# Up projection of a gated MLP on one Trainium2 core: eight of 22 column pairs made from seven half-size products, with sums on VectorE

## The chip, the cores and the metric

The kernel runs on one core of a Trainium2 chip. Its time is the device time of one execution in microseconds (us). A run is one such time; a kernel's time is the median of its runs. One further execution is taken under the hardware profiler, and every row shown below comes from it. The engines are TensorE (PE, with its weight loads as PEld), VectorE (DVE), ScalarE (ACT), GpSimd (POOL) and SyncE (SP), whose queue issues all the large DMAs of this kernel.

## The reference, cut to what matters

One layer of a trunk with D = 1024, 512 tokens and an inner width of 2816. Token mixing comes first and is not touched. The second half of the layer is:

```python
h = rmsnorm(x) * (1 + scale) + shift          # (512, 1024), adaLN
u = causal_dwconv(h @ w_up)                   # w_up (1024, 5632), width 3 along the tokens
gate, value = split(u, 2)                     # 2816 columns each
x = x + adaLN_gate * ((silu(gate) * value) @ w_down)
```

## The kernel before, in words

Inputs and outputs are float32. The kernel splits each operand of this projection into a high part (a cast to the type that the rows call fp32r) and a low part (the operand less its high part), and a product is made of three matmuls, high by high, low by high and high by low, each with 128 rows of K.

The up projection is the loop over f from 0 to 21 (L1302). Pair f is the gate tile f and the value tile f+22, each 128 columns of `w_up` by 512 tokens. `up` (L1287 to L1293) makes one tile in a PSUM bank: 8 K-tiles by 3 matmuls of 512 tokens, so 48 matmuls a pair. In each of its halves of K the weights come through `load_w`: SP loads 256 KB into `w_st` (three buffers), ACT casts it to `w_hi` (L225), POOL subtracts to get `w_lo` (L227); `w_hi` and `w_lo` have nine slots each, so weights can be ready about two pairs ahead. Pairs 0 and 1 are made in halves of 256 tokens, out of four banks, while the last rows of `h2_hi` and `h2_lo` (the split of h, transposed) come in.

`conv` (L1295 to L1300) follows for each tile: ACT scales it out of PSUM (L1297), DVE adds the two shifted terms (L1298, L1299), each of which reads the bank again. Then ACT takes Silu of the gate (L1325), DVE multiplies (L1326), ACT casts (L1327) and DVE makes the low part (L1328) of the activation, which the down projection reads later. Banks go round a ring of eight (L1282).

At f = 4 and 8 the second adaLN gate is summed on DVE (`gate_steps`, seven L410 rows each), from 256 KB pieces that SP loads between the weights; at f = 6 and 10 it is split, at f = 7 and 11 TensorE sums it over partitions (`gate_end`, L421) and DVE adds it to `g2b` (L423).

The down projection (`down`, L1174 to L1201) loads its weights with `share` 2: every second low part is made on DVE and not on POOL. Each engine takes its instructions in the order in which the program holds them.

Of the kernel before, what the change touches and what calls it, by code (L numbers as in the profile page):

```python
# [27 lines left out]
NF = D_FF // P  # L28
# [108 lines left out]
def hybrid_trunk(ctx, tc, x, vecs, convs, mod_cols, mod_gates, in_first, in_cols, in_fox, in_moba, fox_f_bias, lora,  # L137
                 rwkv_g2, w_out, w_up, w_down, norm_final, out):
    nc = tc.nc
    mm = nc.tensor.matmul  # L140
    V, S, G = nc.vector, nc.scalar, nc.gpsimd
    dma = nc.sync.dma_start
# [76 lines left out]
    def split_w(staged, share=0):  # L219
        st, nkt, n = staged  # L220
        pool, bufs = wpools[0] if len(wpools) == 1 or turn[0] % sum(b for _, b in wpools) < 3 else wpools[1]
        turn[0] += 1
        hi = pool.tile([P, WCOLS], F32R, name="w_hi", bufs=bufs)
        lo = pool.tile([P, WCOLS], F32R, name="w_lo", bufs=bufs)
        (V.tensor_copy if hv[0] else S.copy)(hi[:, :n], st[:, :n])  # L225
        e = V if share and turn[0] % share == 0 else G
        e.tensor_tensor(lo[:, :n], st[:, :n], f32(hi[:, :n]), op=OP.subtract)  # L227
        return [z[:, :n].rearrange("p (k n) -> p k n", k=nkt) for z in (hi, lo)]
# [69 lines left out]
    with tc.manual_schedule(engines=ENGINES):  # L298
# [9 lines left out]
        n = vrows.shape[0]  # L308
# [11 lines left out]
        for k in range(NK):  # L320
            mm(pc[k // 4][:, P * (k % 4):P * (k % 4) + P], cact[:, k:k + 1].to_broadcast([P, P]), ident,
               start=True, stop=True)
# [18 lines left out]
        for k in range(NK):  # L341
# [29 lines left out]
            hi, lo = wk[k]  # L371
            for w, h, last in ((hi, hT_hi, False), (lo, hT_hi, False), (hi, hT_lo, True)):
                for j in range(NFIRST):
                    mm(first[j], w[:, P * j:P * j + P], h[:, k, :], start=k == 0 and w is hi and not last,  # L374
                       stop=k == NK - 1 and last)
# [112 lines left out]
    with mix:  # L488
# [294 lines left out]
        with tc.tile_pool(name="bounce", bufs=1) as bp, tc.tile_pool(name="abp", bufs=1, space=PSUM) as abp, \  # L783
# [10 lines left out]
            for s in range(31):  # L794
                m, w = s + 1, 31 - s
# [285 lines left out]
        for cc in range(NC_):  # L1081
# [19 lines left out]
            pu = bank("ch", [P, 4, 64])  # L1101
# [8 lines left out]
            if cc < NC_ - 1:  # L1110
                pn = bank("ch", [P, 4, 64])
                for j in range(4):
                    for par in range(2):
                        mm(pn[H[par], j, :], BKT[:, j, cc, 64 * par:64 * par + 64], vs[cc][:, par, j, :],
                           start=True, stop=True)
# [37 lines left out]
    late = ctx.enter_context(tc.tile_pool(name="late", bufs=1))  # L1153
    g2b = consts.tile([P, D], F32, name="g2b", tag="cB")
    h2_hi = late.tile([P, NK, T], F32R, name="h2_hi")
    h2_lo = late.tile([P, NK, T], F32R, name="h2_lo")
    def tm(dt=F32):
        return late.tile([P, T], dt, name="tm", bufs=TM)
# [110 lines left out]
    feed.run(UP2)  # L1269


    a_hi = [hbuf.tile([P, NK, T], F32R, name="h_hi"), late.tile([P, NF - NK, T], F32R, name="a_hi")]
    a_lo = [hbuf.tile([P, NK, T], F32R, name="h_lo"), late.tile([P, NF - NK, T], F32R, name="a_lo")]

    def act_tile(arr, f):
        return arr[0][:, f, :] if f < NK else arr[1][:, f - NK, :]

    def cvec(w, f):
        n = 44 * w + f
# [2 lines left out]
    ring = itertools.cycle(("mm", "ch", "at", "mm", "ch", "at", "pv", "ch"))  # L1282

    def up_weights(f):
        return [load_w(w_up[f, q], 4) for q in range(2)]
# [9 lines left out]
    def conv(pu, f):  # L1295
        u = tm()
        S.activation(u, pu, AF.Identity, scale=cvec(2, f), bias=cvec(3, f))  # L1297
        V.scalar_tensor_tensor(u[:, 1:], pu[:, 0:T - 1], cvec(1, f), u[:, 1:], op0=OP.mult, op1=OP.add)  # L1298
        V.scalar_tensor_tensor(u[:, 2:], pu[:, 0:T - 2], cvec(0, f), u[:, 2:], op0=OP.mult, op1=OP.add)  # L1299
        return u  # L1300

    for f in range(NF):  # L1302
        if f == 0:

            pfirst = [bank(t) for t in ("ch", "ch", "at", "at")[:2 * FG]]
            for h in range(2):
                for n, pu in enumerate(pfirst):
                    feed.run(max(0, 6 + 2 * n - len(kept)))
                    up(pu, kept[4 + 2 * n:6 + 2 * n], slice(256 * h, 256 * h + 256))
                    if h == 0 and n < 2:  # L1310
                        norm2_cols(2 + n)
            us = [conv(pu, n // 2 + NF * (n % 2)) for n, pu in enumerate(pfirst[:2])]
        elif f < FG:
            us = [conv(pu, f + NF * n) for n, pu in enumerate(pfirst[2 * f:2 * f + 2])]
        else:
            us = []
            for z in (f, f + NF):
                pu = bank(next(ring))
                up(pu, up_weights(z), slice(0, T))
                us.append(conv(pu, z))  # L1320
        ug, uv = us
        if f == 0:
            LATE.close()
            mixers.close()
        S.activation(ug, ug, AF.Silu)  # L1325
        V.tensor_tensor(uv, ug, uv, op=OP.mult)  # L1326
        S.copy(act_tile(a_hi, f), uv)  # L1327
        V.tensor_tensor(act_tile(a_lo, f), uv, f32(act_tile(a_hi, f)), op=OP.subtract)  # L1328
        if f == 2:
            dma(g2b, gate_bias(40))  # L1330
            nfb = consts.tile([P, D], F32, name="nfb", tag="g1b")
            dma(nfb, norm_final[None, :].to_broadcast([P, D]))
        if f in (4, 8):
            for g in gate_steps(1, f // 8, tm, tm):
                g()
        if f in (6, 10):
            gate_parts(1, f // 10, tm)
        if f in (7, 11):
            gate_end(1, f // 11, bank(next(ring)), g2b)
# [81 lines left out]
```

## Time and profile before

| | |
|---|---|
| time, median of 3 runs | 747.79 us (746.29 to 749.0) |
| the profiled execution's own time | 747.43 us |
| its span, first to last instruction | 745.7 us |
| mean granted TensorE clock | 0.983 |
| pairs 2 to 15, from 396 to 553 us | 157.0 us, PE busy in all of it |

The span is the time between the first and the last instruction; the run is 1.7 us longer. A chain of waits follows the work that ended last back to the start, so its rows are in order of time on one path through the engines. Where a row of instructions says "idle before", it was waiting for what is named behind the arrow.

### The profile page before, as it was taken

What the parts mean: (1) busy time and instruction counts of PE and PEld (TensorE: products, weight loads), DVE (VectorE), ACT (ScalarE), POOL (GpSimd) and SP (SyncE); (2) the same over time, 40 slices, a digit from 0 to 9 for tenths busy, and PEclk for the clock granted to TensorE, in tenths of its full rate; (3) what the DMA queues carried; (4) which work ended last, traced back from release to release, by engine and by line L of the source; (5) the groups of instructions that cost most, each with busy time, mean ns of one, the idle gap of its engine ahead of it and who ended that gap; (6) DMA issues with size and microseconds to landing.
All of it is one profiled execution on the core that took longest, in us unless ns stands there. A gap on an engine that the chain in (4) does not pass through costs nothing.

```text
span 745.7 us, 11381 instructions
## 1 busy us (share of the span) xinstructions
PE 717.4 (96%) x4224; PEld 563.3 (76%) x4224; DVE 422.4 (57%) x761; ACT 350.5 (47%) x671; POOL 300.1 (40%) x262
## 2 busy tenths in 40 slices
PE   6999999999988999999999999999999999999996
PEld 5874767897656766668798888888888888888884
DVE  7957997885997577643645484664344453114114
ACT  8748655454442553535565444354444443223204
POOL 0023744665352312626476544444544522225200
PEclk9999979999997999999999999999999999999998
DMA  8941201337763231214234353633233333232203
GB/s 323 394 165 42 68 19 29 86 100 225 241 193 121 63 123 44 69 46 130 82 100 127 110 178 109 202 102 93 86 102 96 88 107 103 85 99 100 86 13 113
DMA packets 43018, 86.90 MB, mean 117 GB/s; under 512 B 5001, under 2 KB 5203, under 8 KB 42963
## 3 DMA queue, kind: packets, MB, share of 16 engines
q1 hardware_dynamic: 42963, 86.18, 36.4%
q8 instruction: 33, 0.54, 0.3%
q14 instruction: 22, 0.18, 0.1%
HBM read 84.05 MB, written 2.10 MB: 116 GB/s over the span
## 4 chain that ended last, share of the span: by engine, by line
PE 85%; DVE 9%; ACT 2%; issue 1%; DMA 1%; POOL 0%; SPq 0%; DVEq 0%; POOLq 0%; ACTq 0%
PE ch L1290 4%; PE ch L1293 4%; PE ch L1291 4%; PE mm L455 3%; PE at L1290 3%; PE at L1293 3%; PE mm L1290 3%; PE mm L1293 3%; PE at L1291 3%; PE mm L1291 3%; PE mm L456 2%; PE mm L457 2%; PE ch L374 2%; PE ch L1185 2%; PE ch L1184 2%; PE ch L1183 2%
## 5 line engine op out<-in xcount | busy, mean ns | idle before, releaser
L227 POOL TENSOR_TENSOR w_lo<-w_st,w_hi 128x512 fp32r<-128x512 f32 (+1 forms) x164 | 220.1, 1346 | 340.1 <-ACT w_hi L225 318.6
L225 ACT CAST w_hi<-w_st 128x512 fp32r<-128x512 f32 (+1 forms) x184 | 112.9, 617 | 167.9 <-PE at L1185 44.7
L227 DVE TENSOR_TENSOR w_lo<-w_st,w_hi 128x512 fp32r<-128x512 f32 x22 | 16.1, 734 | 83.8 <-ACT w_hi L225 83.8
L1290 PE MATMUL ch<-h_hi,w_hi 128*128 128x512 f32 (+1 forms) x152 | 55.2, 372 | 1.3 <-ACT h_hi L1234 1.3
L1291 PE MATMUL ch<-h_hi,w_lo 128*128 128x512 f32 (+1 forms) x152 | 54.9, 369 | 0.0
L455 PE MATMUL mm<-h_hi,w_hi 128*128 128x512 f32 x104 | 48.8, 469 | 1.8 <-ACT ptr L1017 1.8
L456 PE MATMUL mm<-h_lo,w_hi 128*128 128x512 f32 x104 | 42.2, 406 | 0.0
L457 PE MATMUL mm<-h_hi,w_lo 128*128 128x512 f32 x104 | 42.2, 405 | 0.0
L1290 PE MATMUL at<-h_hi,w_hi 128*128 128x512 f32 (+1 forms) x104 | 36.2, 360 | 0.0
L1291 PE MATMUL at<-h_hi,w_lo 128*128 128x512 f32 (+1 forms) x104 | 36.1, 359 | 0.0
L1293 PE MATMUL ch<-h_lo,w_hi 128*128 128x512 f32 (+1 forms) x152 | 35.0, 371 | 0.0
L1290 PE MATMUL mm<-h_hi,w_hi 128*128 128x512 f32 x88 | 34.7, 394 | 0.0
L1291 PE MATMUL mm<-h_hi,w_lo 128*128 128x512 f32 x88 | 34.6, 393 | 0.0
L1290 PEld LDWEIGHTS ch<-h_hi,w_hi 128*128 128x128 f32 x152 | 28.6, 188 | 7.1 <-ACT h_hi L1234 1.8
L1298 DVE SCALAR_TENSOR_TENSOR tm<-ch,vec,tm 128x511 f32<-128x511 f32 x17 | 12.7, 749 | 36.7 <-ACT tm L1297 36.7
L1291 PEld LDWEIGHTS ch<-h_hi,w_lo 128*128 128x128 f32 x152 | 28.6, 188 | 5.2
L430 DVE SCALAR_TENSOR_TENSOR w_m<-w_m,cB 128x512 f32<-128x512 f32 x32 | 25.8, 831 | 9.7 <-DMA w_m<-in_mod_cols_dram 9.6
L1293 PEld LDWEIGHTS ch<-h_lo,w_hi 128*128 128x128 f32 x152 | 26.7, 188 | 5.5 <-POOL h_lo L1235 0.2
L455 PEld LDWEIGHTS mm<-h_hi,w_hi 128*128 128x128 f32 x104 | 20.3, 195 | 9.0 <-issue 3.1
L1006 ACT ACTIVATE pr<-at,mx 128x128 f32<-128x128 f32 (+3 forms) x32 | 16.9, 527 | 21.6 <-DVE mx L1004 21.1
L1325 ACT ACTIVATE tm<-tm 128x512 f32<-128x512 f32 x22 | 13.9, 633 | 25.6 <-DVE tm L1299 25.6
L1004 DVE TENSOR_REDUCE mx<-at 128x1 f32<-128x128 f32 (+3 forms) x32 | 15.6, 488 | 17.3 <-PE at L1001 17.1
(472 smaller groups left out, 1850.3 us busy)
## 6 DMA issues: line engine op xcount, KB each, us to landing
w_st<-in_w_up_dram SPq DMA_DIRECT2D x88, 256.0 KB, 2.7
w_st<-in_w_down_dram SPq DMA_DIRECT2D x44, 256.0 KB, 2.6
wm<-in_mod_cols_dram SPq DMA_DIRECT2D x16, 512.0 KB, 10.0
w_m<-in_mod_cols_dram SPq DMA_DIRECT2D x32, 256.0 KB, 3.7
w_st<-in_in_cols_dram SPq DMA_DIRECT2D x30, 256.0 KB, 2.7
w_m<-in_mod_gates_dram SPq DMA_DIRECT2D x16, 256.0 KB, 3.0
w_st<-in_w_out_dram SPq DMA_DIRECT2D x16, 256.0 KB, 2.6
tm<-in_mod_gates_dram SPq DMA_DIRECT2D x16, 256.0 KB, 4.7
```

Source lines behind the costliest of these rows:

```text
L225: (V.tensor_copy if hv[0] else S.copy)(hi[:, :n], st[:, :n])
L227: e.tensor_tensor(lo[:, :n], st[:, :n], f32(hi[:, :n]), op=OP.subtract)
L374: mm(first[j], w[:, P * j:P * j + P], h[:, k, :], start=k == 0 and w is hi and not last, stop=k == NK - 1 and last)
L430: V.scalar_tensor_tensor(wm, wm, 1.0, cB[:, cols], op0=OP.mult, op1=OP.mult, accum_out=acc2[:, z, k, half:half + 1])
L455: mm(out[0], hi[:, z, :], hT_hi[:, k, :], start=k == 0, stop=False)
L456: mm(out[0], hi[:, z, :], hT_lo[:, k, :], start=False, stop=False)
L457: mm(out[0], lo[:, z, :], hT_hi[:, k, :], start=False, stop=k == NK - 1)
L1004: V.reduce_max(mx[:, 0:1], s_ps[:, :n], axis=AX.X, negate=True)
L1006: S.activation(pr[:, :n], s_ps[:, :n], AF.Exp, bias=mx[:, 0:1], accum_out=mx[:, 1:2])
L1290: mm(pu[:, tok], hi[:, k % 4, :], h2_hi[:, k, tok], start=k == 0, stop=False)
L1291: mm(pu[:, tok], lo[:, k % 4, :], h2_hi[:, k, tok], start=False, stop=False)
L1293: mm(pu[:, tok], w[k // 4][0][:, k % 4, :], h2_lo[:, k, tok], start=False, stop=k == NK - 1)
```

## The change

Pairs 5, 6, 8, 9, 11, 12, 14 and 15 are made by `up_seven`. It sees a pair as a two by two block product: the two halves of K, the two halves of the tokens, and the gate and value columns. Four half-size blocks of the weights (`a11`, `a12`, `a21`, `a22`) and of h make the result in seven products in place of eight. Each product has 4 K-tiles by 3 matmuls of 256 tokens; so 84 matmuls of 256 replace 48 of 512. The blocks of h are summed and differenced once, by `half_sums` at f = 2 and 3 (tiles `s`, `a0`, `a1`, `a2`, high and low). The weights of such a pair are combined on DVE in place in their staging tiles `w_st4`, which have four buffers, just the four tiles of one pair; seven split weights come of them, with `share` 2. Three partial results are copied out of PSUM by ACT (`snap`, `snap5`) and two adds on DVE put them together in PSUM. The arrays that hold the activations from pair 16 on are allocated later.

```diff
+SEVEN = (5, 6, 8, 9, 11, 12, 14, 15)
+NA = 16
...
+    sums = [[late.tile([P, 4, 256], F32R, name=n + p) for p in ("hi", "lo")] for n in ("s", "a0", "a1", "a2")]
...
+    def half_sums(c):
+        x = {}
+        for q in range(2):
+            for h in range(2):
+                x[q, h] = tm().rearrange("p (k t) -> p k t", k=2)
+                part = (slice(0, P), slice(4 * q + 2 * c, 4 * q + 2 * c + 2), slice(256 * h, 256 * h + 256))
+                (V if h else G).tensor_tensor(x[q, h], f32(h2_hi[part]), f32(h2_lo[part]), op=OP.add)
+        t1, t3, t2, t4 = x[0, 0], x[0, 1], x[1, 1], x[1, 0]
+        V.tensor_tensor(t1, x[0, 1], x[0, 0], op=OP.subtract)
+        V.tensor_tensor(t3, x[1, 1], x[0, 1], op=OP.subtract)
+        V.tensor_tensor(t2, x[1, 1], t1, op=OP.subtract)
+        V.tensor_tensor(t4, x[1, 0], t2, op=OP.subtract)
+        for z, t in zip(sums, (t1, t2, t3, t4)):
+            S.copy(z[0][:, 2 * c:2 * c + 2, :], t)
+            G.tensor_tensor(z[1][:, 2 * c:2 * c + 2, :], t, f32(z[0][:, 2 * c:2 * c + 2, :]), op=OP.subtract)
+
+    def up_seven(f, pu):
+        st = {}
+        for z, q in ((0, 0), (1, 0), (1, 1), (0, 1)):
+            st[z, q] = late.tile([P, T], F32, name="w_st4", bufs=4)
+            dma(st[z, q], w_up[f + NF * z, q])
+
+        def parts(x):
+            return split_w((x, 4, T), 2)
+
+        def product(o, w, x, start, stop):
+            hi, lo = w
+            for k in range(4):
+                mm(o, hi[:, k, :], x[0][k], start=start and k == 0, stop=False, skip_group_check=not start)
+                mm(o, lo[:, k, :], x[0][k], start=False, stop=False, skip_group_check=not start)
+            for k in range(4):
+                mm(o, hi[:, k, :], x[1][k], start=False, stop=stop and k == 3, skip_group_check=not start)
...
+        a11, a12, a21, a22 = st[0, 0], st[0, 1], st[1, 0], st[1, 1]
+        snap, snap5 = tm(), tm()
+        product(pu[1][:, h0], parts(a11), tokens(0, 0), True, True)
+        S.copy(snap[:, h0], pu[1][:, h0])
+        V.tensor_tensor(a11, a11, a21, op=OP.subtract)
+        V.tensor_tensor(a21, a21, a22, op=OP.add)
+        w22 = parts(a22)
+        product(pu[0][:, h0], parts(a12), tokens(1, 0), True, True)
+        V.tensor_tensor(a22, a22, a11, op=OP.subtract)
+        product(pu[1][:, h0], parts(a22), combined(1), False, True)
+        S.copy(snap[:, h1], pu[1][:, h0])
+        V.tensor_tensor(a12, a12, a22, op=OP.subtract)
+        product(pu[0][:, h1], parts(a21), combined(0), True, True)
+        S.copy(snap5[:, h0], pu[0][:, h1])
+        product(pu[1][:, h0], parts(a11), combined(2), False, True)
+        V.tensor_tensor(pu[1][:, h1], pu[1][:, h0], snap5[:, h0], op=OP.add)
+        product(pu[0][:, h1], parts(a12), tokens(1, 1), False, True)
+        V.tensor_tensor(pu[0], pu[0], snap, op=OP.add)
+        product(pu[1][:, h0], w22, combined(3), False, True)
...
+        elif f in SEVEN:
+            pu = [bank(next(ring)) for z in range(2)]
+            up_seven(f, pu)
+            us = [conv(pu[z], f + NF * z) for z in range(2)]
...
+        if f in (2, 3):
+            half_sums(f - 2)
```

In the changed kernel the same statements stand lower: `w_lo` is L230, the shifted adds of `conv` are L1368 and L1369, the product with Silu L1402, the activation's low part L1404, the gate's pieces L406 to L426. The four combinations of weights are L1332, L1333, L1336 and L1339, and the two adds in PSUM L1343 and L1345.

The order of DVE's instructions before, from the value tile of pair 10 to the first shifted add of pair 12:

```order
L1298 SCALAR_TENSOR_TENSOR tm<-at,vec_108,tm 128x511
L1299 SCALAR_TENSOR_TENSOR tm<-at,vec_108,tm 128x510
L1326 TENSOR_TENSOR tm<-tm 128x512
L1328 TENSOR_TENSOR a_lo<-tm,a_hi 128x512
L1298 SCALAR_TENSOR_TENSOR tm<-mm,vec_108,tm 128x511
L1299 SCALAR_TENSOR_TENSOR tm<-mm,vec_108,tm 128x510
L423 TENSOR_TENSOR g2b<-g2b,at 128x512
L1298 SCALAR_TENSOR_TENSOR tm<-ch,vec_108,tm 128x511
L1299 SCALAR_TENSOR_TENSOR tm<-ch,vec_108,tm 128x510
L1326 TENSOR_TENSOR tm<-tm 128x512
L1328 TENSOR_TENSOR a_lo<-tm,a_hi 128x512
```

The same engine after, from the value tile of pair 10 to the first add in PSUM of pair 11 (the staging tiles of pair 11 are `w_st_5351` to `w_st_5357`; `w_st_5500` to `w_st_5506` are pair 12's):

```order
L1369 SCALAR_TENSOR_TENSOR tm<-at,vec_108,tm 128x510
L1336 TENSOR_TENSOR w_st_5355<-w_st_5355,w_st_5351 128x512
L1402 TENSOR_TENSOR tm<-tm 128x512
L1339 TENSOR_TENSOR w_st_5357<-w_st_5357,w_st_5355 128x512
L230 TENSOR_TENSOR w_lo<-w_st_5355,w_hi 128x512
L1404 TENSOR_TENSOR a_lo<-tm,a_hi 128x512
L230 TENSOR_TENSOR w_lo<-w_st_5351,w_hi 128x512
L426 TENSOR_TENSOR g2b<-g2b,at 128x512
L230 TENSOR_TENSOR w_lo<-w_st_5500,w_hi 128x512
L1332 TENSOR_TENSOR w_st_5500<-w_st_5500,w_st_5502 128x512
L1343 TENSOR_TENSOR ch<-ch,tm 128x256
```

The combinations and low parts of pair 11 have come in between the conv rows of pair 10, and the first two DVE instructions on pair 12's weights stand ahead of pair 11's own add in PSUM.

SP's queue before, from pair 8 on (the gate's eight pieces between the weights, then the rest of `w_up`):

```order
L216 DMA w_st<-in_w_up_dram 128x512 x14
L403 DMA tm<-in_mod_gates_dram 128x512
L216 DMA w_st<-in_w_up_dram 128x512 x2
L403 DMA tm<-in_mod_gates_dram 128x512 x7
L216 DMA w_st<-in_w_up_dram 128x512 x40
```

SP's queue after, the loads of pair 11, of the gate's second half and of pair 12:

```order
L1308 DMA w_st_5351<-in_w_up_dram 128x512
L1308 DMA w_st_5353<-in_w_up_dram 128x512
L1308 DMA w_st_5355<-in_w_up_dram 128x512
L406 DMA tm<-in_mod_gates_dram 128x512
L219 DMA w_st<-in_w_up_dram 128x512
L1308 DMA w_st_5357<-in_w_up_dram 128x512
L219 DMA w_st<-in_w_up_dram 128x512
L406 DMA tm<-in_mod_gates_dram 128x512 x7
L219 DMA w_st<-in_w_up_dram 128x512 x2
L1308 DMA w_st_5500<-in_w_up_dram 128x512
L1308 DMA w_st_5502<-in_w_up_dram 128x512
L1308 DMA w_st_5504<-in_w_up_dram 128x512
L1308 DMA w_st_5506<-in_w_up_dram 128x512
```

The loads of pair 11 stand ahead of those of pair 10 and of the gate's pieces, and the loads of pair 12 follow at the end, each into the buffer that a tile of pair 11 leaves.

## Rows read from the trace of the kernel before

**Rows 1.** Profile page, part 1, busy time, share and instructions by engine.

```profile
PE 717.4 (96%) x4224; PEld 563.3 (76%) x4224; DVE 422.4 (57%) x761; ACT 350.5 (47%) x671; POOL 300.1 (40%) x262
```

**Rows 2.** Profile page, part 4, the chain that ended last, by engine.

```profile
PE 85%; DVE 9%; ACT 2%; issue 1%; DMA 1%; POOL 0%; SPq 0%; DVEq 0%; POOLq 0%; ACTq 0%
```

**Rows 3.** Windows: before the loop, pairs 2 to 15, the end.

```profile
core 0: us, PE busy (x) PEld busy (x) DVE busy (x) ACT busy (x) POOL busy (x), PEclk, DMA share, GB/s
365.00:375.00 10.00, 7.49 (x60) 7.10 (x60) 7.63 (x15) 6.79 (x17) 5.77 (x6) 1.00 0.23 58
396.00:553.00 157.00, 157.00 (x678) 127.23 (x677) 81.65 (x106) 71.21 (x114) 76.33 (x58) 1.00 0.42 124
736.00:745.00 9.00, 2.45 (x11) 1.65 (x9) 3.22 (x6) 3.25 (x8) 0.00 (x0) 0.77 0.35 132
```

**Rows 4.** Chain of waits in the up projection: start us, us, what.

```profile
377.60 0.94 PE at L1293 x8
...
391.73 0.95 PE at L1293 x8
...
401.95 1.87 PE ch L1293 x8
...
614.43 1.86 PE ch L1293 x8
```

**Rows 5.** Lines by form, PE: gate ends within the loop, busy, mean ns.

```profile
L421 PE MATMUL ch<-tm,ones 128*128 128x512 f32 x2 | 0.6, 395 | 0.0
```

**Rows 6.** Lines by form, DVE: two inputs from SBUF.

```profile
L1326 DVE TENSOR_TENSOR tm<-tm 128x512 f32<-128x512 f32 x22 | 17.6, 800 | 1.2 <-ACT tm L1325 0.4
L227 DVE TENSOR_TENSOR w_lo<-w_st,w_hi 128x512 fp32r<-128x512 f32 x22 | 16.1, 734 | 83.8 <-ACT w_hi L225 83.8
...
L1328 DVE TENSOR_TENSOR a_lo<-tm,a_hi 128x512 fp32r<-128x512 f32 x14 | 9.7, 692 | 8.5 <-ACT a_hi L1327 8.5
```

**Rows 7.** Lines by form, DVE: one input from PSUM.

```profile
L1298 DVE SCALAR_TENSOR_TENSOR tm<-ch,vec,tm 128x511 f32<-128x511 f32 x17 | 12.7, 749 | 36.7 <-ACT tm L1297 36.7
...
L918 DVE TENSOR_TENSOR KR<-KR,ch 128x256 f32<-128x256 f32 x8 | 3.3, 418 | 1.3 <-PE ch L917 1.2
...
L1206 DVE TENSOR_TENSOR ch<-ch,g2b 128x512 f32<-128x512 f32 x3 | 2.1, 697 | 0.9 <-PE ch L1185 0.9
```

**Rows 8.** Lines by form, ACT.

```profile
L225 ACT CAST w_hi<-w_st 128x512 fp32r<-128x512 f32 x180 | 110.4, 617 | 166.2 <-PE at L1185 44.7 <-PE ch L1293 24.6 <-PE ch L1185 23.7
...
L1297 ACT ACTIVATE tm<-ch,vec 128x512 f32<-128x512 f32 x17 | 13.2, 776 | 4.2 <-PE ch L1293 3.2 <-DVE tm L410 1.0
```

**Rows 9.** Lines by form, POOL.

```profile
L227 POOL TENSOR_TENSOR w_lo<-w_st,w_hi 128x512 fp32r<-128x512 f32 x160 | 214.0, 1342 | 336.9 <-ACT w_hi L225 315.5 <-PE ch L525 8.0 <-PE pv L457 5.8
```

**Rows 10.** Timeline of DVE at pairs 4 and 5: start us, us.

```profile
427.75 0.75 DVE L1299 SCALAR_TENSOR_TENSOR tm<-at,vec,tm 128x510 f32<-128x510 f32 x1
...
437.23 1.71 DVE L410 SCALAR_TENSOR_TENSOR tm<-tm,cact 128x512 f32<-128x512 f32 x1
```

**Rows 11.** Timeline of POOL, same stretch.

```profile
427.52 1.30 POOL L227 TENSOR_TENSOR w_lo<-w_st,w_hi 128x512 fp32r<-128x512 f32 x1 [0.27 <-ACT w_hi L225]
...
437.09 1.30 POOL L227 TENSOR_TENSOR w_lo<-w_st,w_hi 128x512 fp32r<-128x512 f32 x1 [2.56 <-ACT w_hi L225]
```

**Rows 12.** Timeline of DVE in the mixing, both engines queued.

```profile
86.37 0.68 DVE L638 TENSOR_TENSOR BK<-kv,s 128x512 f32<-128x512 f32 x1
86.97 0.68 DVE L639 TENSOR_TENSOR KR<-KR,P 128x512 f32<-128x512 f32 x1
...
90.29 1.78 DVE L633 TENSOR_TENSOR KR<-kk,P 128x512 f32<-128x512 f32 x1
91.99 1.75 DVE L635 TENSOR_TENSOR BK<-a,s 128x512 f32<-128x512 f32 x1
```

**Rows 13.** Timeline of POOL, same stretch.

```profile
91.48 1.71 POOL L631 TENSOR_TENSOR kv<-kv,t 128x512 f32<-128x512 f32 x1
```

**Rows 14.** Profile page, part 6: DMA issues, KB each, us to landing.

```profile
w_st<-in_w_up_dram SPq DMA_DIRECT2D x88, 256.0 KB, 2.7
```

More of the change, by code (lines that the diff above doesn't have):

```diff
@@ L1269, in hybrid_trunk @@
     feed.run(UP2)
-    a_hi = [hbuf.tile([P, NK, T], F32R, name="h_hi"), late.tile([P, NF - NK, T], F32R, name="a_hi")]
-    a_lo = [hbuf.tile([P, NK, T], F32R, name="h_lo"), late.tile([P, NF - NK, T], F32R, name="a_lo")]
+    a_hi = [hbuf.tile([P, NK, T], F32R, name="h_hi"), late.tile([P, NA - NK, T], F32R, name="a_hi")]
+    a_lo = [hbuf.tile([P, NK, T], F32R, name="h_lo"), late.tile([P, NA - NK, T], F32R, name="a_lo")]
+    sums = [[late.tile([P, 4, 256], F32R, name=n + p) for p in ("hi", "lo")] for n in ("s", "a0", "a1", "a2")]
@@ L1275, in act_tile @@
     def act_tile(arr, f):
-        return arr[0][:, f, :] if f < NK else arr[1][:, f - NK, :]
+        if f >= NA and len(arr) < 3 + (f - NA) // 2:
+            arr.append(late.tile([P, 2, T], F32R, name=f"a{(f - NA) // 2}" + ("hi" if arr is a_hi else "lo")))
+        return arr[0][:, f, :] if f < NK else arr[1][:, f - NK, :] if f < NA else arr[2 + (f - NA) // 2][:, f % 2, :]
+    def half_sums(c):
[13 more added lines that the diff above has]
+            G.tensor_tensor(z[1][:, 2 * c:2 * c + 2, :], t, f32(z[0][:, 2 * c:2 * c + 2, :]), op=OP.subtract)
@@ new lines, in up_seven, with tokens, combined @@
+    def up_seven(f, pu):
[12 more added lines that the diff above has]
+                mm(o, hi[:, k, :], x[1][k], start=False, stop=stop and k == 3, skip_group_check=not start)
+        def tokens(q, h):
+            return [[z[:, 4 * q + k, 256 * h:256 * h + 256] for k in range(4)] for z in (h2_hi, h2_lo)]
+        def combined(n):
+            return [[sums[n][i][:, k, :] for k in range(4)] for i in range(2)]
+        h0, h1 = slice(0, 256), slice(256, 512)
+        a11, a12, a21, a22 = st[0, 0], st[0, 1], st[1, 0], st[1, 1]
[17 more added lines that the diff above has]
+        product(pu[1][:, h0], w22, combined(3), False, True)
```

## The prediction, made before the result was known

> **What bounds the kernel now.** I read the page first. TensorE is busy for 96% of the span [rows 1], and of the chain that ended last 85% lies on it, 9% on DVE, 2% on ACT and nothing on POOL or the queues [rows 2]. That is a mean over stages, so I next read the window of the pairs that the change touches or prepares, 2 to 15: from 396 to 553 us TensorE is busy for 157.0 of 157.0 us at full clock, while DVE has 81.65 us of work, ACT 71.21, POOL 76.33, and the DMAs 0.42 [rows 3]. In this stretch TensorE is the bound and the vector engines run at about half load. So a matmul removed there is worth its whole time, as long as nothing else comes to end later; and what DVE and POOL take on is free up to about 70 us each, if it can be laid between TensorE's demands.
>
> **What is removed on TensorE.** The chain of waits gives prices of one matmul without the records' overlap. From 377.60 to 391.73 it passes five groups of 24 matmuls of 256 tokens [rows 4]: 14.13 / 120 = 117.8 ns each. From 401.95 to 614.43 it passes 38 groups of 24 with 512 tokens, and the two gate ends, four matmuls of the same width [rows 4, 5]: 212.48 / (38 x 24 + 4) = 232.0 ns. A pair of 48 x 232.0 = 11.13 us becomes 84 x 117.8 = 9.90 us. Half-size matmuls cost hardly more than half, so of the ideal eighth (1.39 us) 1.24 us is left. Eight pairs: 9.9 us. With all else hidden the stretch takes 147.1 us and the kernel 747.4 - 9.9 = 737.5 us. (The profiled execution, 747.43 us, is the base of the sums; it is 0.36 us under the median of the three runs, and well inside them.)
>
> **What is added on DVE.** By the nearest rows: 32 combinations of weights (four a pair) and the 12 of the half sums that fall to DVE have the shape of L1326, 0.80 us [rows 6]: 25.6 + 9.6. Of the 56 low parts of weights every second goes to DVE: 28 at 0.69, as L1328 [rows 6], 19.3. The 8 adds of 256 columns in PSUM are like L918, 0.42; the 8 of 512 like L1206, 0.70 [rows 7]: 3.4 + 5.6. Together 63.5 us, which makes 81.65 + 63.5 = 145 us of rows in a stretch that should last 147. Rows overlap a little where the queue is full: the two at 86.37 and 86.97 start 0.60 us apart and are 0.68 long [rows 12]. For some 200 rows that takes 16 us off: 129 us at least.
>
> **What is moved between the others.** ACT gets 24 copies of 256 columns, each at most the 0.62 of a cast of twice the width [rows 8], and 8 casts for the half sums in place of 8 weight casts: 71 becomes at most 86 us, so it stays idle for two fifths. POOL makes 28 low parts where it made 32, and 12 rows for the half sums, all about 1.30 us [rows 9 to 11]: 76.33 - 5.2 + 15.6 = 86.7 us, 0.59 of 147.1. No bytes are added, and one load lands in 2.7 us [rows 14], so DMA bandwidth is not the matter; the order of the loads is (below).
>
> **The two engines hinder each other.** The row at 437.23 is a DVE instruction with two inputs from SBUF. It starts 0.14 us after a POOL row, which ends at 438.39, takes 1.71 us and so ends 0.55 us after POOL [rows 10, 11]. The same is seen in the mixing: the row at 91.99 ends at 93.74, 0.55 us after POOL's [rows 12, 13]. A DVE row whose other input is a PSUM bank (427.75) lies wholly in a POOL row and takes 0.75 us [rows 10, 11], its usual time [rows 7]. The Trainium skill, page "SBUF — State Buffer", section "Who interferes with whom", has a rule for it: a DVE instruction with two SBUF inputs and a GpSimd instruction that reads SBUF take turns at a shared pair of ports, locked for the whole instruction. The trace agrees, 1.71 us against 0.75. It speaks against this change, since 72 of the 88 added DVE rows are of that kind; if nothing could ever be laid side by side, the sum would be that of rival B below, and by plain durations it would be 737.5. Priced from the rows: each of the 72 (32 + 12 + 28) meets POOL busy 0.59 of the time and then waits half of 1.30 us, 0.38; that is 28 us, of which the 0.80 already holds 0.11 for 44 of them, 5. So DVE needs 129 + 23 = 152 us, already 5 over TensorE's 147.
>
> **Idle time that the order forces.** DVE takes rows in order. At the end of each seven-product pair it waits for the last matmul and then for ACT to scale the tile (0.78 [rows 8]); with 0.4 for the two handovers, an estimate, 1.2 us, 8 times: 10 us. `w_st4` holds one pair. At 6, 9, 12 and 15, which follow a pair of their kind, a tile can only be loaded when the one before is consumed, and then comes 2.7 us of load and 0.62 of cast [rows 14, 8], 3.3 us in which DVE's order already has this tile's low part in front (`w_st_5500` ahead of L1343): 4 x 3.3 = 13, of which I take half, 6.5, since part of it falls beside other rows. On the other side some work of the last pairs can run past the stretch: four shifted adds, the product and the low part are 4 x 0.75 + 0.80 + 0.69 = 4.5 us a pair, two pairs 9. So 152 + 10 + 6.5 - 9 = 159.5 us. TensorE waits 159.5 - 147.1 = 12.4, and I add 2 for pairs 5 and 6, whose first low parts queue on POOL behind the 12 half-sum rows (15.6 us). Sum: 747.4 - 9.9 + 14.4 = 751.9.
>
> A check on one place: from pair 9's last add to the first of pair 11 DVE has 24 rows, 16 to 18 us with or without half of the waits, and about 3 us idle; TensorE has there pair 10's matmuls and most of pair 11's, about 16.4 us. DVE is late by 2 to 5 us. There are three such places (6 to 8, 9 to 11, 12 to 14), so 6 to 15 us, which holds the 14.4. **Bounds.** Nothing waits: 737.5. At the other end rows overlap half as much as at 86.37 (8 us back) and the loads cost their whole 13: 152 + 8 + 10 + 13 - 9 = 174, 29 late with the 2 on POOL, 766.
>
> **The rivals.** *B, only the lock counts.* If the order packs well, what can't be laid side by side is POOL's 86.7 us and DVE's two-input rows: 28 products and low parts, 16 of the gate, 72 new, 116 x 0.60 = 70 us. Together 156.3 us against 157.0 now: 746.7 us, no change. For it: nine slots of weights let DVE run two pairs ahead. Against: the order's waits come on top. *C, hidden: faster.* DVE's 129 us fit in 147 if POOL's rows and DVE's mostly miss each other, which the scheduler's order may bring about, and the waits at the ends of pairs fall in DVE's slack of 18 us: 738 to 745, about 741. It decides where locks and waits together stay under that 18; I count 23 + 16.5 - 9 = 30.5. For it speaks that rows 10 to 13 show the loser held up only when both are queued, and POOL waits for ACT between its rows often (idle before w_lo, 315.5 us in all [rows 9]). Against: DVE now feeds ACT and so POOL, so all three bunch up. *D, worse.* Either the chain of one pair's weights, which starts only when the pair before lets the tiles go, is longer than a pair: load 2.7, cast 0.62, low 1.30, two combinations 1.6, cast 0.62, low 0.69 to 1.30, that is 7.5 to 8.1 us plus queueing; at 12 us each of the four pairs that follow one of their kind would be late by 2 more, 8 us: 760, and 757 to 768 round it. Or the waits of TensorE bring its clock down: in the window at 365 it idles 2.5 of 10 us and stays at 1.00, in that at 736 it idles 6.6 of 9 and is at 0.77 [rows 3], so that only waits much longer than mine would do it.
>
> **How the numbers follow.** My forecast, DVE late by some 14 us, has a chance of 0.45, with its own range of 749.7 to 757 us; B 0.20; C 0.22; D 0.13. A difference under 0.3%, 2.2 us, can't be told from none in this kernel. So slower 0.58 (forecast and D), same 0.20 (B), faster 0.22 (C). The time is the forecast's, 752. The range leaves out the best of C and the worst of D, one in ten in all: 741 to 763.
>
> **What would show each step.** TensorE's 84 matmuls a pair near 9.9 us of chain when nothing waits (else the saving is mis-sized). In the stretch from pair 2 to pair 15, DVE near 100% busy by digits of 9, and TensorE idle some 14 us, most of it ended by DVE rows (L1336, L1339, `w_lo` on DVE, L1343). Mean durations of the combinations over 0.80 us, of DVE's `w_lo` in pairs 5 to 15 over 0.69; POOL's about 1.4. The time from pair 16 on unchanged. I am wrong if DVE is under 90% busy there, if TensorE's waits end on DMA or ACT rather than DVE, or if the combinations take 0.7 us because the engines miss each other.

## The result, and the profile after

The changed kernel takes 775.05 us (median of 4 runs, 772.9 to 776.68) where the kernel before took 747.33 (4 runs): a ratio of 1.037, interval 1.033 to 1.040. It is slower, as forecast, but by 27.7 us and not by 4.6, and outside the range. The profiled execution took 776.68 us; the sums below are made against it.

The page of the changed kernel, parts 1, 2 (40 slices of 19.4 us) and 4, answers to [rows 1, 2]:

```profile
PE 727.9 (94%) x4512; PEld 583.3 (75%) x4512; DVE 493.7 (64%) x849; ACT 373.9 (48%) x727; POOL 323.3 (42%) x270
...
PE   7999999999988999999899689889989999999996
...
DVE  6948996886996578525468788899865443114104
...
PEclk9999989999788999999999769999999999999999
...
PE 68%; DVE 13%; issue 5%; POOL 5%; ACT 5%; DMA 3%; SPq 0%; POOLq 0%; DVEq 0%; ACTq 0%
```

The chain that ended last has left TensorE for 17% of the span more, and it went to all the others, not to DVE alone. The digits show where: PE falls to 6 in the 23rd slice and to 8 in several after it, and the granted clock falls with it. The windows from the first matmul of pair 2 to the first of pair 16, and of a piece of it, answer to [rows 3]:

```profile
396.20:578.30 182.10, 162.79 (x967) 144.30 (x966) 149.76 (x193) 92.66 (x167) 98.88 (x65) 0.93 0.31 100
437.00:452.00 15.00, 10.17 (x38) 8.49 (x39) 10.95 (x14) 5.46 (x10) 9.24 (x7) 0.50 0.64 210
```

This stretch takes 182.1 us where it took 156.8 (392.5 to 549.3; the window of 157.0 in [rows 3] lies 3.5 us later). That is 25.2 of the 29.3 us between the two profiled executions. Another 3.7 us had gone before pair 2 began: this start varies with dips of the clock before it, from 390.2 to 399.9 us over all the traces of this case (10.2 us at the lower level go with the first, 34.1 with the last), so from here on I compare stretches. DVE has 149.8 us of rows, close to the 145 of the sum, and is 82% busy: it is not the bound. Against the 147.1 us of the sum 35 are lost. TensorE idles 18.9 us in waits. Most of the other 16 is the clock: from 437.1 to 457.6 us it is 0.50, the lower of the two levels, 1.2 GHz (the second line has a piece of it), and twice more for 3.4 us, which outside the waits costs 11.4 us. Some 5 are left, and go with the waits (last section). The waits of TensorE in the stretch, the six longest of fifteen groups:

```profile
PE pv L1317 <- POOL w_lo L230: 4.7, 1, 4.7
PE mm L1316 <- ACT tm L1331: 2.3, 1, 2.3
PE mm L1361 <- POOL w_lo L230: 1.9, 1, 1.9
PE ch L1316 <- ACT w_hi L228: 1.7, 2, 0.9
PE at L1316 <- ACT tm L1341: 1.5, 1, 1.5
PE mm L1317 <- POOL w_lo L230: 1.4, 1, 1.4
```

Over all fifteen, POOL, which I had not made a bound, ends 8.5 us of the waits and the longest one; ACT, which I had idle for two fifths, ends 7.6, of which 5.9 through the copies out of PSUM (L1331, L1338, L1341); DVE ends 2.8. The longest wait is at pair 5. TensorE there:

```profile
437.43 0.58 PE L1317 MATMUL pv<-shi,w_lo 128*128 128x256 f32 x1 [4.67 <-POOL w_lo L230]
```

POOL ahead of it:

```profile
429.81 4.67 POOL L1301 TENSOR_TENSOR slo<-tm,shi 128x512 fp32r<-128x512 f32 x1 [3.74 <-ACT shi L1300]
434.44 1.71 POOL L1301 TENSOR_TENSOR a1lo<-tm,a1hi 128x512 fp32r<-128x512 f32 x1
436.12 1.26 POOL L230 TENSOR_TENSOR w_lo<-w_st,w_hi 128x512 fp32r<-128x512 f32 x1
```

And DVE beside it:

```profile
429.66 0.68 DVE L1296 TENSOR_TENSOR tm<-tm 128x512 f32<-128x512 f32 x1
430.26 0.68 DVE L1402 TENSOR_TENSOR tm<-tm 128x512 f32<-128x512 f32 x1
430.86 0.68 DVE L1297 TENSOR_TENSOR tm<-tm 128x512 f32<-128x512 f32 x1
431.47 0.68 DVE L230 TENSOR_TENSOR w_lo<-w_st,w_hi 128x512 fp32r<-128x512 f32 x1
432.07 0.68 DVE L1298 TENSOR_TENSOR tm<-tm 128x512 f32<-128x512 f32 x1
432.67 0.68 DVE L1404 TENSOR_TENSOR h_lo<-tm,h_hi 128x512 fp32r<-128x512 f32 x1
433.27 0.74 DVE L1368 SCALAR_TENSOR_TENSOR tm<-ch,vec,tm 128x511 f32<-128x511 f32 x1
```

This is the lock of [rows 10, 11] the other way round. DVE has a row of two-SBUF-input instructions in its queue, none is late (0.68 each), and POOL's row lasts 4.67 us: it ends 1.2 us after DVE comes to a row with a PSUM operand (433.27). The low part that TensorE wants stands behind it. I had charged the lock to DVE alone. The Trainium skill, page "SBUF — State Buffer", section "Who interferes with whom", says that the order of issue decides who blocks. DVE's first row starts 0.15 us ahead of POOL's here, and POOL's 0.14 us ahead of DVE's in [rows 10, 11], so both orders are in the traces of this case.

### The profile page after: what moved, and what is told of

It reads as the page before. It is cut to its first block, busy times and chain, and to the rows that moved or that the text cites. A ratio compares the mean times of both kernels' runs of the same rounds, so it can differ in the third digit from the quotient of the medians.

```text
span 775.0 us, 12128 instructions
## 1 busy us (share of the span) xinstructions
PE 727.9 (94%) x4512; PEld 583.3 (75%) x4512; DVE 493.7 (64%) x849; ACT 373.9 (48%) x727; POOL 323.3 (42%) x270
## 4 chain that ended last, share of the span: by engine, by line
PE 68%; DVE 13%; issue 5%; POOL 5%; ACT 5%; DMA 3%; SPq 0%; POOLq 0%; DVEq 0%; ACTq 0%
POOL w_lo L230 3%; PE mm L458 3%; PE mm L459 3%; PE mm L460 2%; DMA w_st<-in_w_up_dram 2%; PE ch L377 2%; PE ch L1187 2%; PE ch L1186 2%; PE ch L1188 2%; PE mm L377 1%; PE at L377 1%; PE ch L1360 1%; PE ch L1361 1%; PE ch L1363 1%; PE pv L1032 1%
## 5 line engine op out<-in xcount | busy, mean ns | idle before, releaser
L230 POOL TENSOR_TENSOR w_lo<-w_st,w_hi 128x512 fp32r<-128x512 f32 (+1 forms) x160 | 221.5, 1391 | 338.4 <-ACT w_hi L228 299.8
L228 ACT CAST w_hi<-w_st 128x512 fp32r<-128x512 f32 (+1 forms) x208 | 126.2, 618 | 165.6 <-PE at L1188 44.8
L230 DVE TENSOR_TENSOR w_lo<-w_st,w_hi 128x512 fp32r<-128x512 f32 x50 | 44.1, 881 | 93.1 <-ACT w_hi L228 93.0
L458 PE MATMUL mm<-h_hi,w_hi 128*128 128x512 f32 x104 | 49.3, 474 | 1.1 <-ACT ptr L1020 1.1
L460 PE MATMUL mm<-h_hi,w_lo 128*128 128x512 f32 x104 | 42.5, 408 | 0.0
L1360 PE MATMUL ch<-h_hi,w_hi 128*128 128x512 f32 (+1 forms) x104 | 36.3, 361 | 1.4 <-ACT h_hi L1237 1.4
L1361 PE MATMUL ch<-h_hi,w_lo 128*128 128x512 f32 (+1 forms) x104 | 36.0, 358 | 0.0
L1368 DVE SCALAR_TENSOR_TENSOR tm<-ch,vec,tm 128x511 f32<-128x511 f32 x17 | 12.7, 749 | 23.2 <-ACT tm L1367 23.2
L1360 PE MATMUL at<-h_hi,w_hi 128*128 128x512 f32 (+1 forms) x80 | 26.8, 350 | 0.0
L1361 PE MATMUL at<-h_hi,w_lo 128*128 128x512 f32 (+1 forms) x80 | 26.6, 349 | 0.0
L1361 PE MATMUL mm<-h_hi,w_lo 128*128 128x512 f32 x56 | 22.7, 405 | 1.9 <-POOL w_lo L230 1.9
L460 PEld LDWEIGHTS mm<-h_hi,w_lo 128*128 128x128 f32 x104 | 20.4, 196 | 5.0
L1363 PE MATMUL ch<-h_lo,w_hi 128*128 128x512 f32 (+1 forms) x104 | 23.0, 360 | 0.0
L459 PEld LDWEIGHTS mm<-h_lo,w_hi 128*128 128x128 f32 x104 | 20.8, 200 | 2.3
L1360 PE MATMUL mm<-h_hi,w_hi 128*128 128x512 f32 x56 | 22.5, 402 | 0.0
## 6 DMA issues: line engine op xcount, KB each, us to landing
wm<-in_mod_cols_dram SPq DMA_DIRECT2D x16, 512.0 KB, 10.3
```

Source lines behind the costliest of these rows:

```text
L458: mm(out[0], hi[:, z, :], hT_hi[:, k, :], start=k == 0, stop=False)
L459: mm(out[0], hi[:, z, :], hT_lo[:, k, :], start=False, stop=False)
L460: mm(out[0], lo[:, z, :], hT_hi[:, k, :], start=False, stop=k == NK - 1)
L1360: mm(pu[:, tok], hi[:, k % 4, :], h2_hi[:, k, tok], start=k == 0, stop=False)
L1361: mm(pu[:, tok], lo[:, k % 4, :], h2_hi[:, k, tok], start=False, stop=False)
L1363: mm(pu[:, tok], w[k // 4][0][:, k % 4, :], h2_lo[:, k, tok], start=False, stop=k == NK - 1)
```

## The experiments

The matmuls' price first, and which part costs by itself. Ratios are against runs of the kernel before (7 to 17 of them, medians 747.9 to 749.1 us); stretches are from the first matmul of pair 2 to the first of pair 16. **x1** keeps the seven products and the splits; the sums of h, the combinations, the copies and the adds are out, and the third product opens a half bank of its own:

```diff
-            half_sums(f - 2)
-        V.tensor_tensor(a11, a11, a21, op=OP.subtract)
...
-        S.copy(snap[:, h0], pu[1][:, h0])
...
-        V.tensor_tensor(pu[1][:, h1], pu[1][:, h0], snap5[:, h0], op=OP.add)
-        V.tensor_tensor(pu[0], pu[0], snap, op=OP.add)
-            return [[sums[n][i][:, k, :] for k in range(4)] for i in range(2)]
+            return tokens(n // 2, n % 2)
```

> Leaves out: the sums of h, the combinations of weights, the copies out of PSUM and the adds in PSUM; the eight pairs are seven products of plain blocks, 84 matmuls of 256, with seven split weights of which every second low part is on DVE. If the price of the matmuls is right and nothing else holds TensorE, the stretch of pairs 2 to 15 takes 147 us and the kernel 747.4 - 9.9 = 737.5 us, at a clock of 1.00 from pair 2 on. If half-size matmuls or the 28 low parts on DVE cost more than I counted, it stays above 742.

738.41 us, ratio 0.989 (0.982 to 0.995). Its window of pairs 2 to 15:

```profile
398.90:546.00 147.10, 147.10 (x967) 134.22 (x966) 106.14 (x133) 80.55 (x135) 73.60 (x52) 1.00 0.39 122
```

147.1 us as worked out, without a wait. The saving is real, 9.8 us of the 156.8; everything above it is lost elsewhere.

**x2** takes out the half sums alone (the first and the last of the edits of x1), **x3** the four combinations alone (the second), and **x4** makes no pair from seven products but computes the half sums:

```diff
-SEVEN = (5, 6, 8, 9, 11, 12, 14, 15)
+SEVEN = ()
```

> Leaves out: the sums and differences of h (plain blocks of h stand in their place); all else as changed. Theory S (the half sums are 12 rows on POOL in front of the low parts of pairs 5 and 6, TensorE waits 8.8 us there, and that wait brings its clock down): without them the 8.8 us and some 8.5 us of low clock between 437 and 458 us go, so about 775 - 17 = 758. Theory V (DVE's work for all eight pairs is too much, the half sums only show it first): TensorE's waits move to the later pairs and the time is 768 or more.

761.53 us, ratio 1.020 (1.013 to 1.027), stretch 170.3 us, TensorE waits 12.9.

> Leaves out: the four combinations of weights per pair (32 DVE rows, 25.6 us by L1326, 27 us as measured in the changed kernel); all else as changed, the half sums too. Theory S: pairs 5 and 6 keep most of their wait and the low clock, 765 to 770. Theory V: DVE has room again, waits after pair 6 and most of the clock loss go, and the time is 755 or less.

767.08 us, ratio 1.026 (1.020 to 1.032), stretch 171.9, waits 15.3.

> Computes all that the reference asks: no pair is made from seven products, but the half sums of h are computed (and not used). Theory S: POOL's 12 rows and DVE's 12 delay the low parts of pairs 4 to 6 too, but TensorE has 512-column matmuls and weights of two pairs in hand: 748 to 753. If the sums were harmless by themselves: 747 to 748, the time before.

748.51 us, ratio 1.002 (0.999 to 1.005), stretch 156.8 as before, no wait, though POOL is 96.7 us busy in it and DVE 102.6.

Theory S came near in x2 and x3, and yet was not enough. In x4 the other branch holds: the sums are harmless in front of ordinary pairs. In front of the new ones they cost 13.5 us (x2), and 23 us of stretch stay lost without them. Removing either part left some 170 us of stretch. So the cost lies in how the parts meet. The next four ask where.

**x5** leaves out the copies and adds only (the third to fifth removals of x1; the third product has a half bank of its own, as there), **x6** the sums and the combinations, so that copies and adds stay; **x7** is x2 with eight staging buffers; **x8** is meant to fill pair 5's long wait with 30 matmuls:

```diff
-            st[z, q] = late.tile([P, T], F32, name="w_st4", bufs=4)
+            st[z, q] = late.tile([P, T], F32, name="w_st4", bufs=8)
...
+        if f == 5:
+            for k in range(30):
+                mm(pu[1][:, h1], w1[0][:, k % 4, :], h2_hi[:, k % 8, 0:256], start=k == 0, stop=k == 29)
```

The first two lines are x7's, the others x8's, ahead of the third product.

> Leaves out: the three copies out of PSUM and the two adds in PSUM of each of the eight pairs (24 ACT rows, 16 DVE rows); the sums of h and the combinations stay. Theory R (round trips: a product that goes on in a half bank must wait for the copy or add that reads it, with one product of 1.4 us between, and ACT and DVE, in order, come late): the 7.2 us that TensorE waited for these rows and the low clock after them go, and the time is 760 to 765. Theory L (late weights: DVE's and POOL's queues are too full): the low parts still come late, only 9 us of DVE rows are gone, and the time is 768 to 773.

758.62 us, ratio 1.014 (1.011 to 1.017), stretch 168.2, waits 13.8, all on weights and the half sums (4.9 for one low part of these at pair 5). The time is Theory R's, a little better even; the waits that are left are Theory L's.

> Leaves out: the sums of h and the combinations of weights; the copies and adds in PSUM stay, in the order of the changed kernel. Theory R: the waits on copies and adds stay, some 7 us, and low clock after them: 745 to 752. Theory L: with DVE's queue short they are answered in time, and TensorE waits for under 2 us: 738 to 741, as the products alone (738.4).

757.68 us, ratio 1.011 (1.008 to 1.014), stretch 162.5, waits 10.3. Longer than Theory R gave, and DVE had room (the combinations are out). Its TensorE at pair 5, which waits for the add of 256 columns (L1338 in this kernel), and its DVE ahead of that add:

```profile
447.40 0.58 PE L1315 MATMUL ch<-h_hi,w_hi 128*128 128x256 f32 x1 [4.28 <-DVE ch L1338]
```

```profile
436.24 9.09 DVE L413 SCALAR_TENSOR_TENSOR tm<-tm,cact 128x512 f32<-128x512 f32 x7
445.25 1.75 DVE L230 TENSOR_TENSOR w_lo<-w_st,w_hi 128x512 fp32r<-128x512 f32 x1
446.92 0.42 DVE L1338 TENSOR_TENSOR ch<-ch,tm 128x256 f32<-128x256 f32 x1
```

Seven rows of the second gate stand in a block ahead of the add. Before the change they delayed nothing (TensorE has no wait in its stretch): convs wait in the ring of banks. Now pair 5's last product waits behind them. That gave theory G.

> Leaves out: the sums of h; and w_st4 has eight buffers, two pairs. To be held against the run without the half sums and with four buffers (761.5). If the single staging makes the weights late (TensorE waits 5.0 us there for w_lo and w_hi), those waits and the low clock after them go: 750 to 755. If not, 759 to 763.

761.04 us against 761.53: no difference in the time. The stretch is 167.5 us against 170.3 and the waits 11.1 against 12.9, so little comes of it while the gate's block is there.

> Computes all that the reference asks, as the changed kernel, with 30 more matmuls of 256 tokens (3.5 us) put ahead of the third product of pair 5, into a half bank that is not in use yet; TensorE sits idle for 4.67 us there in the changed kernel. If the clock falls because of that idle time: the wait shrinks to some 1.2 us, the clock stays at 1.00 in the 20 us after it, and the time falls by some 8 us, to 767. If the clock there has another cause: no change, 774 to 776, or the low clock stays in the trace.

782.29 us, ratio 1.044 (1.041 to 1.048): a miss, and no test. (In this kernel pair 5's values are not the reference's.) The matmuls did not fill the wait:

```profile
448.53 5.88 PE L1341 MATMUL ch<-h_hi,w_hi 128*128 128x256 f32 x30
```

The scheduler orders the instructions of each kernel anew. In its order for TensorE, here as in the changed kernel, pair 5's product with `s` (the fourth in the source, the one that waits 4.67 us) and work of pair 6 stand ahead of pair 5's third product, so the 30 ran behind all the waits of pair 5. ACT and DVE got another order there too, and TensorE waited longer, 26.8 us in all, 5.05 and 3.89 at 438 and 445 us for casts. The clock is low there as well (0.66 from 425 to 450 us). It doesn't show what the clock would do without idle time.

**x9** moves the second gate behind the eight pairs, **x10** does the same to x6 and **x11** to x2; **x12** has five spaced pairs, with the gate late.

```diff
-        if f in (4, 8):
+        if f in (16, 18):
...
-        if f in (6, 10):
+        if f in (18, 20):
...
-        if f in (7, 11):
+        if f in (19, 21):
...
-SEVEN = (5, 6, 8, 9, 11, 12, 14, 15)
+SEVEN = (7, 9, 11, 13, 15)
```

The three conditions are those of the gate's steps, parts and ends; the last line is x12's.

> Computes all that the reference asks: as the changed kernel, with the second gate's steps at f = 16 and 18 (parts at 18 and 20, ends at 19 and 21), behind the eight pairs, in place of 4 and 8. Theory G (the gate's rows, seven in a row on DVE, stand ahead of the adds in PSUM and the low parts of pairs 5 and 9, which TensorE waits for): the waits near pair 6 and at pair 9 (1.4 + 1.9 + 2.3 us) and the low clock after them go, and the time is 760 to 766; pair 5's wait of 4.7 us stays. Theory H (the half sums alone are the matter, since DVE and POOL shut each other out): 770 to 775.

762.44 us, ratio 1.018 (1.014 to 1.022), stretch 170.7, waits 18.8. The time is Theory G's, but pair 5's wait did not stay at 4.7 us: it is 9.95 (below).

> Leaves out: the sums of h and the combinations, as the run with copies and adds only (757.7), and has the gate's steps behind the eight pairs. Theory G: that run's waits of 4.3 and 3.2 us on the adds in PSUM stood behind the gate's rows; they go, with the low clock after them, and 3 us are left: 740 to 745. Theory R alone (copies and adds come late whatever stands ahead): 750 to 757.

741.76 us, ratio 0.990 (0.987 to 0.993):

```profile
395.60:543.00 147.40, 146.77 (x963) 133.75 (x962) 94.75 (x127) 90.13 (x158) 70.24 (x53) 1.00 0.33 95
```

One wait of 0.63 us is left of 10.3. The time is Theory G's again, and the copies and adds cost next to nothing by themselves (1.3 us against x14, below). But more changed than DVE's queue. With the gate early, TensorE's order in the kernels that have copies and adds mixes products of pair 6 into pair 5; with it late, each pair's products follow one another as in the source. That the gate's rows stood ahead of an add is seen in x6; what the block costs is only shown together with that order.

> Leaves out: the sums of h; the gate's steps stand behind the eight pairs. Held against the run without the sums (761.5). Theory G: 748 to 754. If the combinations with their low parts fill DVE by themselves (theory V): 756 to 761. What it has above 738.4 is the price of the combinations, copies and adds without a burst beside them.

753.02 us, ratio 1.005 (1.003 to 1.007), as Theory G has it:

```profile
393.50:553.00 159.50, 150.34 (x963) 134.53 (x962) 119.80 (x159) 87.53 (x159) 77.01 (x53) 1.00 0.29 88
```

Waits are 8.9 us, at clock 1.00. One of them, TensorE and then ACT (L1330 is the first copy of a pair here, L1366 a conv's scaling):

```profile
464.46 0.39 PE L1315 MATMUL at<-h_hi,w_hi 128*128 128x256 f32 x1 [1.64 <-ACT tm L1330]
```

```profile
460.77 0.62 ACT L228 CAST w_hi<-w_st 128x512 fp32r<-128x512 f32 x1 [2.62 <-DMA w_st<-in_w_up_dram]
461.29 0.77 ACT L1366 ACTIVATE tm<-mm,vec 128x512 f32<-128x512 f32 x1
463.52 0.62 ACT L228 CAST w_hi<-w_st 128x512 fp32r<-128x512 f32 x1 [1.45 <-DMA w_st<-in_w_up_dram]
464.05 0.36 ACT L1330 COPY tm<-at 128x256 f32<-128x256 f32 x1
```

The copy stands on ACT behind a cast of the next pair's weights, whose load could not start before a tile of this pair was done with. x9 has the same at pair 5, larger. There the low part that frees the tile stands on POOL behind two rows of the half sums, of which the first is shut out for 4.67 us, as above; SP issues the next pair's loads 0.02 us after it, ACT waits for the load, and the copy stands behind ACT's cast:

```profile
423.82 4.67 POOL L1301 TENSOR_TENSOR slo<-tm,shi 128x512 fp32r<-128x512 f32 x1 [3.75 <-ACT shi L1300]
428.45 1.71 POOL L1301 TENSOR_TENSOR a1lo<-tm,a1hi 128x512 fp32r<-128x512 f32 x1
430.13 1.26 POOL L230 TENSOR_TENSOR w_lo<-w_st,w_hi 128x512 fp32r<-128x512 f32 x1
431.41 3.99 SPq L1308 DMA_DIRECT2D w_st<-in_w_up_dram  x4
433.98 0.62 ACT L228 CAST w_hi<-w_st 128x512 fp32r<-128x512 f32 x1 [3.56 <-DMA w_st<-in_w_up_dram]
436.17 0.36 ACT L1331 COPY tm<-ch 128x256 f32<-128x256 f32 x1
436.59 0.58 PE L1316 MATMUL ch<-a0hi,w_hi 128*128 128x256 f32 x1 [9.95 <-ACT tm L1331]
```

> Computes all that the reference asks: five pairs from seven products, every other one, 7, 9, 11, 13 and 15, the gate's steps behind them. If bursts and not the mean load are the matter, the sums are done before pair 7, and every such pair has an ordinary one before it to load and combine its weights: five times 1.24 us are saved and 2 to 3 us waited for, 743 to 746. If the round trips and the lock cost 1.5 us or more a pair whatever stands round them: 749 to 754.

763.41 us, ratio 1.018 (1.015 to 1.022): the worst miss. Five pairs take as long as eight with the gate late (762.44, x9): stretch 166.7, where five savings with nothing lost would leave 149.7 (156.8 - 0.9 for the gate ends - 6.2), waits 11.8. TensorE at pair 7, and ACT before it:

```profile
460.61 0.38 PE L1316 MATMUL mm<-a0hi,w_hi 128*128 128x256 f32 x1 [4.04 <-ACT tm L1331]
```

```profile
454.47 0.62 ACT L1403 CAST h_hi<-tm 128x512 fp32r<-128x512 f32 x1 [2.03 <-DVE tm L1402]
...
457.96 0.63 ACT L1401 ACTIVATE tm<-tm 128x512 f32<-128x512 f32 x1 [1.16 <-DVE tm L1369]
...
459.00 0.77 ACT L1367 ACTIVATE tm<-ch,vec 128x512 f32<-128x512 f32 x1
...
460.19 0.37 ACT L1331 COPY tm<-mm 128x256 f32<-128x256 f32 x1
```

An ordinary pair ahead is no help. ACT still works off the convs of earlier pairs, step by step with DVE, when pair 7's copy is due: TensorE was done with the tile that ACT scales at 459.00 (`ch`) at 453.7, 5.3 us before, and with the one before it 7.4 us before its scaling. The copy stands behind that lag.

The last three ask what of x11's loss is staging, what is the weights, and whether a whole version gains. **x13** is x11 with `bufs=8`, **x14** is x11 without copies and adds, **x15** has all sums, the gate late, and:

```diff
-SEVEN = (5, 6, 8, 9, 11, 12, 14, 15)
+SEVEN = (7, 8, 9, 10, 12, 13, 14, 15)
...
-TM = 8
+TM = 6
...
-            st[z, q] = late.tile([P, T], F32, name="w_st4", bufs=4)
+            st[z, q] = late.tile([P, T], F32, name="w_st4", bufs=6)
```

> Leaves out: the sums of h; the gate's steps stand behind the eight pairs and w_st4 has eight buffers, two pairs. Held against the run with the gate late and four buffers (753.0, TensorE waits 8.9 us, 7.3 of them for copies out of PSUM that stand on ACT behind a cast that waits for its load). If the single staging is what makes those copies late: under 3 us of waits, 742 to 746. If it is DVE's combinations and low parts as such (lock and load): 750 to 754.

748.35 us, ratio 1.001 (0.998 to 1.004), between the two:

```profile
394.30:548.80 154.50, 149.54 (x962) 134.22 (x961) 119.81 (x159) 88.26 (x159) 77.18 (x53) 1.00 0.27 84
```

Waits are 4.7 us. Staging is 4.9 us of x11's 13.3.

> Leaves out: the sums of h, the copies out of PSUM and the adds in PSUM; the gate's steps stand behind the eight pairs; the combinations and four staging buffers stay. If TensorE only loses where a late DVE or ACT row stands ahead of a copy or an add that it waits for: 738 to 742, since late weights have two pairs in hand. If the combined weights themselves come late: 747 to 753.

740.67 us, ratio 0.991 (0.988 to 0.994):

```profile
395.20:541.40 146.20, 146.20 (x963) 133.52 (x962) 119.22 (x143) 80.44 (x134) 74.86 (x52) 1.00 0.30 94
```

No wait at all, with 119 us of DVE rows in 146. Combined weights are not late by themselves; in x5, with the half sums and the gate's block in the queues, they were.

> Computes all that the reference asks: pairs 7 to 10 and 12 to 15 from seven products, the gate's steps behind them, six staging buffers (paid for with two of the eight tm buffers). If bursts and staging are the whole loss, two ordinary pairs more ahead of the first one take up the half sums, and the time is 742 to 748, at or below the kernel before. If the half sums, which POOL and DVE keep from each other, still reach TensorE: 752 to 760.

765.25 us, ratio 1.026 (1.020 to 1.032), stretch 165.5, waits 13.4, the longest again on pair 7's first copy (4.09). Another 5 us go behind the stretch (202.7 us to the end against 197.7 in x9), 2.9 of them in one wait of TensorE for the gate's parts, at 608.1. No version tried beats the kernel before with all of the sums made; x13, which leaves the half sums out, only equals it.

## Why the prediction was wrong in size

Stretches of pairs 2 to 15, in the order in which the parts come together. The base is 146.1, that is 147.1 less the two gate ends, some 0.9 us, that lie behind the stretch where the gate is late. The first three rows are held against the base, the last two each against the row above:

| | stretch | more |
|---|---|---|
| products and combinations (x14) | 146.1 | 0 |
| products, copies and adds (x10) | 147.4 | 1.3 |
| combinations, copies and adds (x11) | 159.5 | 13.3 |
| and half sums (x9) | 170.7 | 11.3 |
| and the gate at 4 and 8 (the changed kernel, less 0.9) | 181.1 | 10.4 |

In the first four TensorE takes the products of pairs 5 and 6 in the source's order. The changed kernel does not, so the last 10.4 us are the gate's block and that order together; which of them costs how much is open.

**What bounds, and the saving: right.** 147.1 us, to the tenth (x1), and 9.8 us saved for the 9.9.

**DVE as the bound: the step that failed.** "So DVE needs 129 + 23 = 152 us" and "TensorE waits 159.5 - 147.1" treat DVE as a pipe that is late when its sum is over TensorE's. The sum was about right (149.8 us of rows), and so was the price of the lock, if a little high: the combinations took 0.83 us on the mean and DVE's `w_lo` 1.00, where the forecast comes to 1.07 for each (0.80 - 0.11 + 0.38 and 0.69 + 0.38). But DVE was 82% busy, where under 90% was named as a sign of being wrong, and ended 2.8 of the 18.9 us of waits; ACT, the other sign, ended 7.6 and POOL 8.5. 119 us of DVE rows cost nothing in x14, and 115 in the stretch of x6 go with 10 us of waits. What counts is how soon one row answers. A product that goes on in a half bank waits for a copy on ACT or an add on DVE, with one product, 1.4 us, in between; whatever stands ahead in those queues becomes TensorE's wait. The prediction has no term for such an answer, and none for a block like the gate's `L413 x7` in front of it.

So the direction came out, and that waits forced by the order of the queues would cause it; that 14.4 us of them were forecast and 18.9 came is partly luck, since most ended elsewhere than on DVE. The low clock (11.4 us outside the waits) and what goes beside the waits (some 5) stood in the sum at nothing.

**The half sums: mis-sized.** I gave them 2 us; they cost 11.3 (x9 against x11, with TensorE's order the same at pairs 5 and 6), and the waits of the changed kernel up to the first ordinary pair behind pairs 5 and 6 come to 8.8 us. I charged the lock to DVE only, and did not follow what lies behind the late POOL row: a staging tile, its load, ACT's cast, a copy.

**Single staging: right in kind.** I took 6.5 us for it; 4.9 is what eight buffers gave back in x13, though by another way, ACT's queue and not DVE's.

**The clock: set aside wrongly.** Rival D had it at "waits much longer than mine"; it fell to 0.50 at 437.1, inside the wait of 4.67 us, and stayed there for 20.5 us with shorter waits in them. Over the stretch the clock was 0.96 to 0.99 in x2, x3, x5, x6, x7, x9, x12 and x15 and 0.93 in x8 and the changed kernel, whose longest waits are 2.4 to 9.95 us, and 1.00 in x1, x4, x10, x11, x13 and x14, which have none or at most 1.64. Each of its 21 falls in those ten kernels comes inside a wait of TensorE or at most 1.4 us behind one, and where x10 has lost the waits of x6 the low clock is gone too. That goes with the waits as its cause; x8, which was to show it by itself, did not.

**The rivals.** B, the lock as a bound on the two engines' sum, would give 156 us; x5, which has all the rows of that sum, took 168.2, and what TensorE waited for was single late rows. C is what x14 and x10 show of each half alone. Of the 0.13 for D, the low clock came true; at 775 us the time lies beyond its range too.

## What to carry to other kernels

Before work is moved to engines with free time, ask not only how busy they are but how long TensorE can do without an answer: buffers that hid a lag of two pairs here were replaced by one product of 1.4 us. Every row that stands ahead of such an answer in an in-order queue, also an unrelated one such as the gate's, then has a price. Test the parts singly and in pairs: two of them cost 0 and 1.3 us here, and together 13. And read in the trace where an edit's instructions ran: each new kernel can get another order, and x8's matmuls came behind the wait that they were to fill.

## What was unexpected of the hardware

POOL can be shut out as DVE can: its row of 1.3 us took 4.67 while DVE issued six rows with two SBUF inputs back to back, and DVE lost nothing; x9 has it again, with the same 4.67 us. And waits cost more than their length: in x13, with the clock at 1.00, 4.7 us of them go with 8.4 us of stretch, some 0.3 us more for each of eleven. The rows show most of it:

```profile
443.63 0.28 PE L1316 MATMUL mm<-h_hi,w_lo 128*128 128x256 f32 x1
443.75 0.63 PE L1318 MATMUL mm<-h_lo,w_hi 128*128 128x256 f32 x4
445.06 0.39 PE L1315 MATMUL ch<-h_hi,w_hi 128*128 128x256 f32 x1 [0.68 <-ACT tm L1337]
445.28 0.28 PE L1316 MATMUL ch<-h_hi,w_lo 128*128 128x256 f32 x1
445.40 0.28 PE L1315 MATMUL ch<-h_hi,w_hi 128*128 128x256 f32 x1
```

In an unbroken run matmuls of 256 start 0.12 us apart and each record lasts 0.28, so they overlap. The last one ahead of a wait is counted as busy for its whole 0.28 (0.16 more), and the second one behind it starts 0.22 after the first (0.10 more): 0.26 us a wait that the list of waits leaves out.
